# Latent attention's shifts found by whole pairs, half of them between the differential heads, and a features-first layout for the first layer's inputs

## The chip, the cores and the metric

The kernel runs on one core of a Trainium2 chip. The metric is the device time in microseconds of one execution. Engines: PE (TensorE: matrix products and transposes into the banks of PSUM), DVE (VectorE), ACT (ScalarE), POOL (GpSimd) and SP (SyncE), which here issues all transfers. Each engine works through its own queue in order; semaphores tie the queues together.

## The reference

Two layers over 1024 latent tokens and 256 context tokens of width 1024. Each layer modulates the tokens with a scale and a shift that come from a conditioning vector, projects them, mixes them with two groups of heads, gates and projects back, and normalises. The first layer is the one the change touches:

```python
sh_l, sc_l, g_l = adaln(c, ada_w[l], ada_b[l])      # silu(c) @ ada_w + ada_b, in three parts
hl = xl * (1.0 + sc_l[:, None]) + sh_l[:, None]
hc = xc * (1.0 + sc_c) + sh_c                       # context tokens
...
# 4 differential heads: two softmaxes over the same keys, subtracted
p = softmax(q1 @ k1.T * DA_SCALE) - lam * softmax(q2 @ k2.T * DA_SCALE)
oa = rms_norm(p @ vd) * subln_g * (1.0 - lam_init)
# 8 latent (MLA) heads, 96 features of query and key
ob = softmax(qm @ km.T * MLA_SCALE) @ vm
y = concat([oa, ob]) * silu(gate)
```

Latent tokens see all 1280 keys, context tokens only the 256 of the context.

## The kernel before

**Stages.** The start (0 to 67 us) loads the conditioning weights, tokens and the first input weights, and builds the modulated tokens as `hhi` and `hlo`, a rounded part and a remainder, with features on the partitions. Then come the first layer's projections, which leave queries, keys, values and gates in memory (`s_qk`, `s_v`, `s_mq`, `s_mk`, `s_kr`, `s_mv`, `s_gate`), its attention (about 460 to 1012 us), its output projection, and the second layer.

**The start.** `load_x` brings tokens in with tokens on the partitions (`xt`), and `modulated` (L279) turns each 128x128 block on PE (L285) before ACT scales and shifts it (L287) and DVE writes the two parts (L289, L290). `ada_first` (L250) makes scale and shift from a block of `ada_w`, 128 columns of each, which arrive as runs of 128 numbers (512 bytes). Small vectors (`c`, biases, gains) come as rows, a transfer for each, and are turned on PE in `load_rows` (L188).

**The attention.** `Plan` (L504) holds tasks with engine, cost, predecessors and the buffers that they take and give. `run` picks the task that can start first by these costs (`on_vector`, `on_scalar`) and emits it; so the costs set the order on every engine, but not the times on the chip. Two kinds of unit are planned:

- `Differential` (L563), one head each, 4 in all, for 8 tiles of 128 queries and one context step. For each tile and each of the two softmaxes PE writes scores of 128 x 1280 into a wide PSUM tile `s` of three banks (L565, L566), DVE finds the row maximum (L1329), and ACT takes the exponential (L1336). DVE scales and combines the two (L579, L580, L585) in pieces of 512, 512 and 256; PE turns the result in blocks of 128 (L1353), ACT or DVE moves the blocks out (`moves`, L518), and PE multiplies by the values (L596). There are two `s` tiles and two single banks `tp`.
- `Latent` (L752), two heads each, 4 pairs in all, in groups of 4, 4 and 2 tiles. Here the scores are made turned, keys on the partitions (`st`, L862 to L864), ACT takes their exponential (L878) at once, and PE multiplies by the values (L898). DVE and POOL add up the probabilities (L889), PE sums them over the keys (L906), and DVE takes the reciprocal (L913) and gates. Since nothing can be subtracted behind the product, the row maximum has to be inside it, as feature 97 of the query's remainder (`ql`, row 96), against a row of ones in the keys.

**The shift.** This maximum is found by `Latent.shifts`, a group ahead of its use: a rough product with the rounded parts alone (L789) into an `s` tile, the maximum on DVE (L797 into `nmx`), one-column transposes of `nmx` on PE (L805), and a copy on ACT into the row of `ql` (L810). The score product of a group waits for it. In the latent stage one wide `s` tile is left, and three single banks `st`.

**Queues.** SP issues the loads of the next head or pair (`load_scores`, `load_values`), the stores, the steps of `bias_tables` and the weights of what follows, in the order of the plan. A load into a buffer that is still in use waits on SP, and so does everything behind it. Units use two sets of buffers in turn.

Of the kernel before, what the change touches and what calls it, by code (L numbers as in the profile page):

```python
# [53 lines left out]
RD = 1  # L54
RM = 1
# [80 lines left out]

@with_exitstack
def hybrid_kernel(ctx, tc, t, out, dbg=None):
# [11 lines left out]
    dma(out=cst, in_=t["cst"])  # L150
# [11 lines left out]
    s_mv = dram.tile([NT, 512], F32, name="s_mv")  # L162
    s_gate = dram.tile([KT, P, NT], F32, name="s_gate")
# [21 lines left out]
    V0 = {}  # L185
    V1 = {}

    def load_rows(spec, where, dst, rows, psum, n=0):  # L188
        n0 = n
        G.memset(rows, 0.0)  # L190
        for key, ap, off, k in spec:
            dma(out=rows[n:n + k, :], in_=row_of(ap, off, k))
            where[key] = n
            n += k
        assert n <= P
        ps = psum.tile([P, 512], F32, name="mm")
        T.transpose(ps[:, :P], rows, ident)
        V.tensor_copy(out=dst[:, n0:n], in_=ps[:, n0:n])

    rows_pool = ctx.enter_context(space(name="rows", bufs=1))  # L200

    def vec_rows0(pool, psum):
        rows = pool.tile([P, P], F32, name="rows")
        load_rows([("c", t["c"][0], 0, 8), ("cc", t["c_ctx"], 0, 8)], V0, vt[0], rows, psum)
# [4 lines left out]
    def vec_rows1(psum):  # L209
        ada_b = t["ada_b"]  # L210
        spec = [("ab0", ada_b[0], 0, 16), ("ab1", ada_b[1], 0, 16),
                ("eg", t["ev_b_in"][0], 1952, 8), ("sub", t["da_subln_g"][0], 0, 1),
                ("qg", t["mla_q_norm_g"][0], 0, 2), ("kg", t["mla_kv_norm_g"][0], 0, 1)]
        rows = rows_pool.tile([P, P], F32, name="rows")
        load_rows(spec, V0, vt[0], rows, psum, 16)
# [274 lines left out]

    def on_vector(n):
        return 0.07 + n / 960

    def on_scalar(n, act=True):
        return (0.15 if act else 0.06) + n / 1200
# [15 lines left out]
    def moves(plan, bank, dst, m, last, cut=3):  # L511
# [10 lines left out]
        return [plan.add("AV", (on_scalar((c1 - c0) * P, False), on_vector((c1 - c0) * P)), partial(move, c0=c0, c1=c1),  # L522
# [8 lines left out]
    class Differential(Unit):  # L531
# [22 lines left out]
        def plan(self, tt):  # L554
# [26 lines left out]

            def combine(cs):
                def emit(_):
# [169 lines left out]
    class Latent(Unit):  # L753
# [24 lines left out]
        def shifts(self, plan, g):  # L778
# [58 lines left out]
            if n * w <= 512:  # L837
                return [context]
# [1733 lines left out]
```

## Time and profile before

| | us |
|---|---|
| median of 3 runs | 1938.26 (1933.92 to 1942.24) |
| profiled execution | 1938.62 |
| its span | 1936.9 |
| PE busy | 1803.0 |
| DVE busy | 1128.5 |
| ACT busy | 728.3 |
| POOL busy | 513.1 |

Busy times of matrix products overlap, since one starts before the one ahead of it has left the array; a busy PE is not PE at its peak. The granted clock of PE is 0.966 over the whole span. "Releasers" in the views name the work that ended an idle time. DVE's and ACT's busy times add up without overlap.

### The profile page before, as it was taken

The numbers are of one execution on the slowest core, as the hardware profiler recorded it, in microseconds if no ns is written. First come the engines' busy times: TensorE is split into PE (matmuls) and PEld (weight loads), VectorE is DVE, ScalarE is ACT, GpSimd is POOL, SyncE is SP. The second block draws the span as 40 slices with busy tenths as digits, with TensorE's granted clock in tenths as the row PEclk, the third lists the DMA queues.
The fourth block names the chain that finished last, engine by engine and source line by source line (L and its number), as shares of the span: only waits on it lengthen the run. The fifth ranks groups of instructions, "written<-read, shape, count | busy, mean of one in ns | idle before, by whom it ended". The sixth has DMA issues, their size and how long they took to land.

```text
span 1936.9 us, 29600 instructions
## 1 busy us (share of the span) xinstructions
PE 1803.0 (93%) x11085; PEld 1504.4 (78%) x11085; DVE 1128.5 (58%) x2116; ACT 728.3 (38%) x1451; POOL 513.1 (26%) x531
## 2 busy tenths in 40 slices
PE   7999999999898889889899989999999998998898
PEld 5898998887787766556557779888898877877786
DVE  3654124314889886676676853665676224666756
ACT  2311014434777545334342312334543224444521
POOL 1433134100012104436233422220111002223444
PEclk9999999999999979899899989999999999999999
DMA  9766524677654265422116342225442366677652
GB/s 288 237 199 217 163 72 126 188 203 184 145 125 107 66 152 156 125 67 62 42 55 209 131 148 74 80 74 185 146 134 84 109 193 172 159 204 191 176 163 87
DMA packets 241589, 275.97 MB, mean 142 GB/s; under 512 B 25042, under 2 KB 201118, under 8 KB 241446
## 3 DMA queue, kind: packets, MB, share of 16 engines
q1 hardware_dynamic: 241446, 274.07, 49.2%
q8 instruction: 88, 1.44, 0.3%
q14 instruction: 55, 0.45, 0.1%
HBM read 193.14 MB, written 87.16 MB: 145 GB/s over the span
## 4 chain that ended last, share of the span: by engine, by line
PE 59%; DVE 11%; DMA 5%; issue 3%; ACT 3%; POOL 1%; SPq 1%; DVEq 0%; POOLq 0%; ACTq 0%
PE mm L390 6%; PE mm L392 6%; PE mm L391 6%; PE tp L898 4%; PE tp L596 3%; PE mm L1985 3%; PE mm L1986 2%; PE mm L1987 2%; PE st L862 2%; PE st L864 2%; PE st L863 2%; PE s L789 2%; PE tp L1353 2%; DVE nm L1329 2%; PE s L565 2%
## 5 line engine op out<-in xcount | busy, mean ns | idle before, releaser
L347 POOL TENSOR_TENSOR wlo<-raw,whi 128x1024 fp32r<-128x1024 f32 (+2 forms) x38 | 91.7, 2414 | 210.7 <-ACT whi L339 207.4
L390 PE MATMUL mm<-whi,hhi 128*128 128x256 f32 (+1 forms) x496 | 147.5, 298 | 0.0
L392 PE MATMUL mm<-whi,hlo 128*128 128x256 f32 (+1 forms) x496 | 146.6, 296 | 0.2 <-DVE hlo L290 0.2
L391 PE MATMUL mm<-wlo,hhi 128*128 128x256 f32 (+1 forms) x496 | 146.4, 295 | 0.0
L1329 DVE TENSOR_REDUCE nm<-s 128x1 f32<-128x1280 f32 x64 | 94.6, 1489 | 53.0 <-PE s L566 51.5
L339 ACT CAST whi<-raw 128x1024 fp32r<-128x1024 f32 (+2 forms) x54 | 55.9, 1036 | 179.5 <-DMA raw<-in_ev_w_in_dram 70.6
L797 DVE TENSOR_REDUCE nmx<-s 128x1 f32<-128x1280 f32 x68 | 100.5, 1485 | 37.0 <-PE s L789 36.5
L2375 POOL TENSOR_SCALAR np<-np,nrz 128x640 f32<-128x640 f32 x64 | 52.0, 816 | 233.4 <-DVE nrz L2372 219.7
L1336 ACT ACTIVATE p<-s,nm 128x1280 f32<-128x1280 f32 x64 | 85.0, 1329 | 35.4 <-DVE nm L1329 30.9
L565 PE MATMUL s<-o 128*128 128x512 f32 (+1 forms) x192 | 79.8, 420 | 18.1 <-ACT p L1336 16.4
L390 PEld LDWEIGHTS mm<-whi,hhi 128*128 128x128 f32 x496 | 94.7, 191 | 2.1 <-issue 1.7
L392 PEld LDWEIGHTS mm<-whi,hlo 128*128 128x128 f32 x496 | 94.6, 191 | 0.5 <-DVE hlo L290 0.4
L391 PEld LDWEIGHTS mm<-wlo,hhi 128*128 128x128 f32 x496 | 94.7, 191 | 0.2
L1985 PE MATMUL mm<-h,whi 128*128 128x512 f32 x192 | 78.9, 411 | 3.3 <-DVE hv L2021 3.3
L789 PE MATMUL s<-o 96*128 96x512 f32 (+1 forms) x204 | 65.4, 430 | 17.8 <-DVE nmx L797 11.2
L878 ACT ACTIVATE pt<-st 128x512 f32<-128x512 f32 (+1 forms) x88 | 50.7, 578 | 75.1 <-PE st L864 70.9
L596 PE MATMUL tp<-v,pt 128*128 128x128 f32 x640 | 76.8, 276 | 0.7 <-ACT pt L518 0.2
L596 PEld LDWEIGHTS tp<-v,pt 128*128 128x128 f32 x640 | 74.4, 192 | 3.7 <-DVE pt L518 2.4
L1986 PE MATMUL mm<-h,whi 128*128 128x512 f32 x192 | 76.5, 398 | 0.0
L1987 PE MATMUL mm<-h,wlo 128*128 128x512 f32 x192 | 76.4, 398 | 0.0
L2368 ACT ACTIVATE np<-np,nnm 128x640 f32<-128x640 f32 x64 | 52.9, 827 | 56.4 <-DVE nnm L2362 51.0
L862 PE MATMUL st<-o 96*128 96x512 f32 (+1 forms) x176 | 73.1, 415 | 0.0
(488 smaller groups left out, 5370.1 us busy)
## 6 DMA issues: line engine op xcount, KB each, us to landing
adaw<-in_ada_w_dram SPq DMA_DIRECT2D x16, 1024.0 KB
raw<-in_od_w_in_dram SPq DMA_DIRECT2D x32, 512.0 KB
o<-s_qk SPq DMA_DIRECT2D x48, 320.0 KB
raw<-in_ev_w_in_dram SPq DMA_DIRECT2D x18, 512.0 KB
bt<-s_bt SPq DMA_DIRECT2D x16, 576.0 KB
adaw<-in_ada_w_dram SPq DMA_DIRECT2D x16, 512.0 KB
o<-s_mq SPq DMA_DIRECT2D x16, 480.0 KB
s_gate<-e SPq DMA_DIRECT2D x24, 256.0 KB
```

What stands on the lines that cost most here:

```text
L390: T.matmul(ps, ahi(k), bhi(k), start=k == k0, stop=False)
L391: T.matmul(ps, ahi(k), blo(k), start=False, stop=False)
L392: T.matmul(ps, alo(k), bhi(k), start=False, stop=k == nk - 1)
L565: T.matmul(s[:, n0:n0 + nn], ql, self.kh[b][:, ks], start=True, stop=False)
L596: T.matmul(o[:, :P], x["pt"][:, c, :], self.v[:, k0 + c, :], start=c == 0, stop=c == nch - 1)
L789: T.matmul(x["s", a, i][:, n0:n0 + nn], self.qh[a][0:96, (t0 + i) * P:(t0 + i + 1) * P], self.kh[a][0:96, k0 * P + n0:k0 * P + n0 + nn], s ...
L797: V.tensor_reduce(out=x["m", a][:, i:i + 1], in_=x["s", a, i][:, :w], axis=AX.X, op=ALU.max, negate=True)
L862: T.matmul(st[:, :nq], self.kh[a][0:96, ks], self.qh[a][0:96, qs], start=True, stop=False)
L1329: V.tensor_reduce(out=nm, in_=s[:, :w], axis=AX.X, op=ALU.max, negate=True)
L1985: T.matmul(ps, ah, bh, start=k == 0, stop=False)
L1986: T.matmul(ps, ah, bl, start=False, stop=False)
L1987: T.matmul(ps, al, bh, start=False, stop=k == KT - 1)
```

## The change

Three things are changed.

**1. Shifts.** `Latent.shifts` now works on one head `a` of a pair, over all ten tiles. It reads the rounded queries and keys from memory into tiles of its own: keys into the ring of weights (`whi` for the first, `wlo` for the second head of a pair), queries two tiles at a time into `rq` (three buffers, 40 loads). The maxima of both heads gather in `kept` (128 x 20); one transpose turns them, one copy moves them out, and one transfer writes them to `s_sh` in memory, from where `load_scores` brings the row of `ql` in. Hence a pair is loaded after its rows are written, and the score products wait for no shift of their own. There are 72 such steps in all. The first 36 (pairs 0 and 1) are planned one by one between the 36 steps of the differential heads, the other 36 between the score steps of pairs 0 and 1. Both wide `s` tiles exist from the start; one is given up for three `st` banks when the differential scores are done, and the other when the last shift step is done, for three more. The weights of the next layer begin to load only then. (Before, four steps of pair 0's first group were planned twice: 68 maxima over 1280 keys for 64 tiles.)

**2. Balance.** The middle piece of each combination (512 of 1280) goes from DVE to POOL, as two instructions; blocks that PE has turned are moved out by ACT alone; products over one `s` tile stay together; and the plan's costs of DVE and ACT are raised for this stage.

**3. Layouts.** The host hands over `tokens` (features first), `ada0` (the first layer's `ada_w` in blocks, so that half a block is a transfer of 4 KB runs), and `vectors0` and `vectors1` (small vectors as columns). The 80 transposes of tokens and the three of vectors are gone, and tokens come in 2 KB runs (1 KB for context).

```diff
+    tokens = np.concatenate([inputs["x"][0], inputs["ctx"][0]], axis=0)
+    out["tokens"] = np.ascontiguousarray(tokens.T)
+    w = inputs["ada_w"][0][:, 0:2 * D].reshape(KT, P, 2, KT, P)
+    out["ada0"] = np.ascontiguousarray(w.transpose(3, 1, 0, 2, 4).reshape(KT, P, KT * 2 * P))
...
-        return [plan.add("AV", (on_scalar((c1 - c0) * P, False), on_vector((c1 - c0) * P)), partial(move, c0=c0, c1=c1),
+        return [plan.add("A" if plan.name == "attention" else "AV", (on_scalar((c1 - c0) * P, False), on_vector((c1 - c0) * P)), partial(move, c0=c0, c1=c1),
...
+                    if eng is G:
+                        G.tensor_scalar(out=p2, in0=p2, scalar1=x["ratio"], scalar2=1.0, op0=ALU.mult, op1=ALU.mult)
+                        G.tensor_tensor(out=p1, in0=p1, in1=p2, op=ALU.add)
+                    else:
+                        V.scalar_tensor_tensor(out=p1, in0=p2, scalar=x["ratio"], in1=p1, op0=ALU.mult, op1=ALU.add)
...
+            for n0, nn in pieces(w):
+                eng, cost = ("G", 2.1) if n0 == 512 else ("V", 0.06 + on_vector(nn))
...
+            dma(out=self.ql[a][96:97, :].bitcast(F32), in_=s_sh[p][a:a + 1, :])
...
+        def shifts(self, plan, a):
...
+            def load_q(i):
                 def emit(_):
+                    x["q", i] = rough.tile([P, 256], FR, name="rq", bufs=RQ)
+                    dma(out=x["q", i][0:96, :].bitcast(F32), in_=s_mq[0][2 * self.p + a][:, i * 256:(i + 1) * 256])
...
+            def turn(_):
+                x["t"] = taken("tp")
+                T.transpose(x["t"][0:2 * TILES, 0:P], self.kept.rearrange("p a t -> p (a t)"), ident)
...
+                self.shift.append(plan.add("V", on_vector(n * w), top(tt, n), last, [], ["s"], rank=RM))
+                if tt + n == TILES and a == 1:
+                    last = plan.add("P", 0.2, turn, self.shift, ["tp"])
+                    last = plan.add("A", on_scalar(P, False), rows, [last], ["yd"], ["tp"])
+                    self.rows = plan.add("D", 1.0, store, [last], [], ["yd"])
+            return loading, [partial(step, tt, 1) for tt in range(LT)] + [partial(step, LT, 2)]
...
-                    m = plan.add("P", 3 * nq / 2250, block(c, a), [self.ready[a], self.shift[g, a]], ["st"],
+                    m = plan.add("P", 3 * nq / 2250, block(c, a), [self.ready[a]], ["st"],
...
+                h = xp.tile([P, 512], F32, name="h", bufs=3)[:, :n * P]
+                S.activation(out=h, in_=xs[g, k // 2][:, k % 2, :], func=AF.Identity,
...
+        usual = dict(fixed)
+        fixed.update(V=0.15, copy=0.16)
...
+            after = [u.rows] if u in mla else []
...
+        parts_left = [(j, step) for j, (_, steps) in enumerate(ahead) for step in steps]
+        parts_later = parts_left[9 * EARLIER:]
+        parts_left = parts_left[:9 * EARLIER]
...
+                for j, step in parts_left[:-(-len(parts_left) // units_left)]:
+                    step()
...
+                for j, later in parts_later[:1]:
+                    later()
...
+                    if len(parts_later) == 1:
+                        plan.add("P", 0.01, banks, [plan.tasks[-1]], ["s"], ["st"] * 3)
+                        spread(plan, w1.begin(), [plan.tasks[-2]])
```

Line numbers in the rows of after are those of the changed file: L830 is the rough product, L839 its maximum, L888 to L890 the score products, L610 the combination on DVE, L607 and L608 that on POOL.

On PE, where pair 0 ends and pair 1 begins, before stood the values (L898) and sums (L906) of the last group, rough products into the one wide tile (`s_4838`), four one-column transposes, a rough product more, and then the scores:

```order
L898 MATMUL tp_4840<-p_4841,v 64x256 x2
L898 MATMUL tp_4840<-pt_4847,v 64x256 x2
L906 MATMUL tp_4839<-oo,cst 64x256 x2
L789 MATMUL s_4838<-o_7004 128x512 x2
L789 MATMUL s_4838<-o_7004 128x256
L805 MATMUL tp_4839<-cst,nmx 1x128 x4
L789 MATMUL s_4838<-o_7054 128x512 x2
L789 MATMUL s_4838<-o_7054 128x256
L862 MATMUL st_7098<-o_7004 128x512
```

Now, at the same place, the sums (L932) stand between score products of the next pair (the other operands `o_7803` and `o_7741` are its loaded tiles):

```order
L888 MATMUL st_7083<-o_7741 128x512
L889 MATMUL st_7083<-o_7741 128x512
L890 MATMUL st_7083<-o_7741 128x512
L932 MATMUL tp_4715<-oo,cst 64x256 x2
L888 MATMUL st_7081<-o_7803 128x512
L889 MATMUL st_7081<-o_7803 128x512
L890 MATMUL st_7081<-o_7803 128x512
```

The transposes and the rough products ahead of the first scores are gone from between the pairs.

On DVE, in a differential head, a tile before was two maxima, the ratio and three pieces (`x2` are the first two):

```order
L1329 TENSOR_REDUCE nm<-s_4856 128x1
L1329 TENSOR_REDUCE nm<-s_4838 128x1
L579 RECIPROCAL ratio<-zs 128x1
L580 SCALAR_TENSOR_TENSOR ratio<-ratio,r_5354,nlam 128x1
L585 SCALAR_TENSOR_TENSOR p_4843<-p_4844,ratio,p_4843 128x512 x2
L585 SCALAR_TENSOR_TENSOR p_4843<-p_4844,ratio,p_4843 128x256
```

Now two pieces are left of the combination, and the maximum of a latent tile (`kept`) follows them:

```order
L1355 TENSOR_REDUCE nm<-s_4713 128x1
L1355 TENSOR_REDUCE nm<-s_4709 128x1
L598 RECIPROCAL ratio<-zs 128x1
L599 SCALAR_TENSOR_TENSOR ratio<-ratio,r_5299,nlam 128x1
L610 SCALAR_TENSOR_TENSOR p_4717<-p_4718,ratio,p_4717 128x512
L610 SCALAR_TENSOR_TENSOR p_4717<-p_4718,ratio,p_4717 128x256
L839 TENSOR_REDUCE kept<-s_4713 128x1
```

A piece of 512 has left DVE and a reduction over 1280 has come in its place.

On SP, in the differential heads, the loads of queries for the shifts (`rq`) now stand between the table's transfers (L1411), the loads of the next head's values and gate (L569, L571), a store of a pair's rows (L854) and the stores of the heads (L770):

```order
L822 DMA rq<-s_mq_70 96x256
L854 DMA s_sh_77<-yd 20x128
L569 DMA v<-s_v 128x10x128
L571 DMA gt<-s_gate 128x1280
L770 DMA s_y<-yd 128x512
L822 DMA rq<-s_mq_70 96x256 x2
```

A query load behind the gate's load (L571) or a store (L770) is issued only when these have been.

More of the change, by code (lines that the diff above doesn't have):

```diff
@@ L162, in hybrid_kernel @@
     s_mv = dram.tile([NT, 512], F32, name="s_mv")
+    s_sh = [dram.tile([2, NT], F32, name=f"s_sh{p}") for p in range(4)]
     s_gate = dram.tile([KT, P, NT], F32, name="s_gate")
@@ L183, in hybrid_kernel, with vectors, vec_rows0 @@
     subg = subgt[:, 0:1]
[L185 to L204, printed above, removed]
+    V0, V1 = [places(spec)[0] for spec in VECTORS]
+    def vectors(i, n0, n1):
+        dma(out=vt[i][:, n0:n1], in_=t[f"vectors{i}"][:, n0:n1])
+    def vec_rows0():
+        vectors(0, 0, 16)
         G.memset(sil, 0.0)
@@ L207, in vec_rows0, with vec_rows1 @@
         S.activation(out=sil[:, :, 1], in_=vt[0][:, 8:16], func=AF.Silu)
[L209 to L215, printed above, removed]
+    def vec_rows1():
+        vectors(0, 16, places(VECTORS[0])[1])
         V.tensor_scalar(out=subgt, in0=vt[0][:, V0["sub"]:V0["sub"] + 1], scalar1=1.0 - (0.8 - 0.6), scalar2=None,
@@ L580, in scale, with emit @@
                 V.scalar_tensor_tensor(out=ratio, in0=ratio, scalar=x["z", 0], in1=nlam, op0=ALU.mult, op1=ALU.mult)
+            x["left"] = len(pieces(w))
             def combine(cs):
[L583 removed]
+                def emit(eng):
                     p1, p2 = x["p", 0][:, cs], x["p", 1][:, cs]
[L585 to L586 removed]
+                    if eng is G:
[3 more added lines that the diff above has]
+                        V.scalar_tensor_tensor(out=p1, in0=p2, scalar=x["ratio"], in1=p1, op0=ALU.mult, op1=ALU.add)
+                    x["left"] -= 1
+                    if not x["left"]:
                         given("p", x["p", 1])
@@ L776, in load_values, with load @@
             dma(out=self.gate, in_=s_gate[4 + p])
-        def shifts(self, plan, g):
-            t0, n = TG[g]
-            k0, w = keys_of(t0)
+        def shifts(self, plan, a):
             x = {}
-            self.shift = getattr(self, "shift", {})
-            def rough(a, i, n0, nn):
+            def load(_):
+                x["k"] = ring[0].tile([P, KT, WC], FR, name=("whi", "wlo")[a]).rearrange("p k n -> p (k n)")[:, :NT]
+                dma(out=x["k"][0:64, :].bitcast(F32), in_=s_mk[0][self.p, 64 * a:64 * a + 64, :])
+                dma(out=x["k"][64:96, :].bitcast(F32), in_=s_kr[0])
+            def load_q(i):
@@ L848, in shifts @@
-            return [partial(step, a, i) for a in range(2) for i in range(n)]
+                    if self.kept is None:
+                        self.kept = at.tile([P, 2, TILES], F32, name="kept", bufs=2)
+                    w = keys_of(tt)[1]
+                    V.tensor_reduce(out=self.kept[:, a, tt:tt + n], in_=x["s", tt][:, :n * w].rearrange("p (m k) -> p m k", k=w),
+                                    axis=AX.X, op=ALU.max, negate=True)
+                    given("s", x["s", tt])
+                return emit
@@ L1478, in hybrid_kernel @@
                 loaded(mla[u.p + 1])
-            ahead = groups[i + 1][0].shifts(plan, groups[i + 1][1]) if i + 1 < len(groups) else []
-            steps = u.scores(plan, g)
-            for c, step in enumerate(steps):
+            for step in u.scores(plan, g):
                 first = len(plan.tasks)
```

198 lines of the change are left out of this document (102 added, 96 removed).

## The prediction

> **What bounds the kernel now.** The first view is the table by stage: busy time of each engine in each stretch, number of instructions in brackets, then the granted TensorE clock, the share of the DMA engines and what they moved.
>
> ```profile
> core 0: us, PE busy (x) PEld busy (x) DVE busy (x) ACT busy (x) POOL busy (x), PEclk, DMA share, GB/s
> 0.00:67.00 67.00, 51.95 (x429) 42.39 (x430) 28.29 (x69) 20.05 (x28) 11.49 (x17) 1.00 1.01 281
> 67.00:460.00 393.00, 388.99 (x2758) 356.68 (x2757) 131.82 (x279) 96.00 (x189) 107.55 (x133) 1.00 0.56 172
> 460.00:722.00 262.00, 227.93 (x1477) 194.33 (x1475) 219.28 (x336) 166.19 (x408) 34.01 (x62) 0.94 0.54 123
> 722.00:1012.00 290.00, 269.28 (x1213) 169.33 (x1213) 195.98 (x189) 120.91 (x216) 122.33 (x101) 0.93 0.31 87
> ```
>
> The change reaches three of these stretches. In the first 67 us the DMA share is 1.01: loading bounds it. From 67 to 460 the PE is busy for 389 of 393 us and nothing is changed there, so what the start gains is carried through. From 460 to 722 (differential heads) no engine is full; VectorE is the fullest by its own work. From 722 to 1012 (latent pairs) PE is idle for 20.7 us, and at a clock of 0.93 it loses another 0.07 x 290 = 20.3 us.
>
> Next I read who PE waited for in these two stretches (total, times, longest), and the clock at one change of pair.
>
> ```profile
> PE s L789 <- DVE nmx L797: 9.6, 7, 2.2
> PE tp L805 <- DVE nmx L797: 8.2, 7, 1.9
> PE tp L906 <- DVE rz L913: 2.7, 3, 0.9
> ...
> PE s L565 <- ACT p L1336: 16.4, 15, 1.9
> ...
> 864.00:877.00 13.00, 10.33 (x32) 7.54 (x33) 8.75 (x9) 2.96 (x5) 1.18 (x1) 0.61 1.03 252
> ```
>
> The first two rows (17.8 of the 20.7 us) are the shift: rough product, maximum on VectorE, transpose, row, and only then the first score product of the next group. They fall where one pair ends and the next begins, and there the clock goes down as well (0.61 in those 13 us). So the latent stage is bound by PE's own stream plus one serial chain that is paid at each change of pair.
>
> **Latent stage.** PE's stream is priced by starts, not by durations (these overlap).
>
> ```profile
> 774.91 0.40 PE L862 MATMUL st<-o 96*128 96x512 f32 x1
> 775.15 0.40 PE L863 MATMUL st<-o 96*128 96x512 f32 x1
> 775.38 0.40 PE L864 MATMUL st<-o 97*128 97x512 f32 x1
> ...
> 777.01 0.28 PE L862 MATMUL st<-o 96*128 96x256 f32 x1
> 777.13 0.28 PE L863 MATMUL st<-o 96*128 96x256 f32 x1
> ...
> 740.03 4.44 PE tp L898 x20
> ...
> L862 PE MATMUL st<-o 96*128 96x512 f32 x160 | 68.5, 428 | 0.0
> L898 PE MATMUL tp<-p,v 128*64 128x512 f32 x160 | 41.5, 597 | 0.0
> L789 PE MATMUL s<-o 96*128 96x512 f32 x96 | 36.7, 463 | 9.6 <-DVE nmx L797 9.6
> L805 PE MATMUL tp<-cst,nmx 128*1 128x128 f32 x65 | 12.3, 298 | 9.0 <-DVE nmx L797 8.2 <-DVE nmx L824 0.8
> L596 PE MATMUL tp<-v,pt 128*128 128x128 f32 x40 | 4.8, 275 | 0.0
> ```
>
> (Counts that no row here shows are of the same list.) A 512-column score product starts every 0.235 us, a 256-column one every 0.12, a value product every 4.44/20 = 0.222. What stays: 480 x 0.235 + 48 x 0.12 (scores) = 118.6; 320 x 0.222 + 32 x 0.12 (values) = 74.9; the sums, 32 x 0.235 + 12 x 0.12 = 9.0; the rest of the last differential head, 40 x 0.12 + 16 x 0.12 = 6.7. Together 209.2 us. Before there stood beside it 96 x 0.235 + 64 x 0.12 = 30.2 us of rough products and about 65 x 0.1 = 6.5 us of one-column transposes, in all 246. The other 44 of the 290 us are the idle time (20.7), the lost clock (20.3) and 3 us that I cannot place.
>
> After: half the rough products are gone from here. The 36 steps left (order of the change) are 32 of 2 x 0.235 + 0.12 = 0.59 us and 4 of 0.24, or 19.9 us; the transposes become 4, after a whole pair, and nothing in the next scores waits for them. So the stream is 209.2 + 19.9 = 229 us. Of the 44 us I leave 11: the 2.7 us for the reciprocal, the 3 unplaced and 5 of the lost clock, since the changes of pair keep their sums and their reciprocals. That makes **240 us, 50 less**. The ends: all 44 stay (273, 17 less), or none (229, 61 less). I lean to the lower end because the waits named are the ones removed. The 36 maxima here cost VectorE 36 x 1.49 = 54 us against 49 before; it is busy for 196 of 290 us, and PE's step of scores, values and rough product (6 x 0.235 + 4 x 0.222 + 0.59 = 2.9 us) covers one maximum, until VectorE falls behind: then PE waits, because only one wide bank is left for the rough products.
>
> **Differential stage.** An undisturbed head, with its groups on VectorE and ScalarE:
>
> ```profile
> 552.90:610.40 57.50, 51.69 (x368) 45.35 (x367) 48.82 (x83) 41.37 (x105) 8.02 (x18) 1.00 0.58 128
> ...
> L585 DVE SCALAR_TENSOR_TENSOR p<-p,ratio,p 128x512 f32<-128x512 f32 x16 | 11.6, 747 | 0.2
> L518 DVE COPY pt<-tp 128x256 f32<-128x256 f32 x7 | 2.9, 420 | 2.3 <-ACT pt L518 2.3
> L518 ACT COPY pt<-tp 128x256 f32<-128x256 f32 x36 | 12.0, 376 | 3.6 <-PE tp L1353 3.4
> ...
> L797 DVE TENSOR_REDUCE nmx<-s 128x1 f32<-128x1280 f32 x49 | 72.8, 1485 | 34.9 <-PE s L789 34.5
> L648 DVE TENSOR_REDUCE nmx<-s 128x4 f32<-128x1024 f32 x4 | 4.9, 1216 | 1.4 <-PE s L643 1.4
> ```
>
> VectorE works 48.8 of 57.5 us. The change takes from it, per head, 8 middle pieces of the combination (8 x 0.747 = 6.0) and 7 copies (2.9), and gives it 8 maxima (8 x 1.485 = 11.9) and one over 512 elements (between 0 and the 1.2 us of the 1024-element row; I take 0.7, near half): 52.5 us. ScalarE takes the copies, 41.4 + 7 x 0.376 = 44 us. PE gets 9 steps, about 5 us. The pieces that go to GpSimd are priced thus:
>
> ```profile
> L726 POOL TENSOR_SCALAR oo<-oo,rs 128x128 f32<-128x128 f32 x32 | 11.3, 372 | 1.0
> ...
> L2375 POOL TENSOR_SCALAR np<-np,nrz 128x640 f32<-128x640 f32 x64 | 52.0, 816 | 233.4 <-DVE nrz L2372 219.7
> ...
> L889 POOL TENSOR_TENSOR oo<-oo,p 128x512 f32<-128x512 f32 x34 | 47.0, 1381 | 46.0 <-ACT p L878 29.9 <-DVE oo L889 13.9
> ...
> 749.38 1.52 POOL L889 TENSOR_TENSOR oo<-oo,p 128x512 f32<-128x512 f32 x1 [0.17 <-ACT p L878]
> ...
> 749.98 1.48 DVE L889 TENSOR_TENSOR oo<-oo,p 128x512 f32<-128x512 f32 x1 [0.22 <-ACT p L878]
> ```
>
> A product with a scalar over 512 is about 0.70 us (between 0.372 and 0.816), an addition 1.38: 2.1 us per tile, 17 per head on an engine that works 8 of 57.5. That is free by itself. It isn't beside VectorE: the last two rows show an addition of VectorE that ran while GpSimd had one and took 1.48 us, about 0.73 more than the 0.747 of the combination alone. VectorE's two remaining pieces run in the same microseconds as GpSimd's two instructions. The price lies between 0 and 2 x 0.73 = 1.46 us per tile; I take 0.5, since the first piece starts before GpSimd and only the second can be held by the 0.70. So 8 x 0.5 = 4: 56.5 us of VectorE.
>
> [...]
>
> Now the idle part: 8.7 us per head today. With a third user of two wide banks more of it is filled, since the maxima need nothing but a bank; I take 6, so 62.5 us per head (ends: 57.5, all new work in today's gaps; 52.5 + 11.7 + 8.7 = 73). Four heads are 250 us against 262, in which the last head already carried 20 rough steps and its own change to the latents: **12 less** (32 less to 30 more).
>
> **The start.**
>
> ```profile
> DMA packets 22994, 15.49 MB, mean 310 GB/s; under 512 B 494, under 2 KB 22990, under 8 KB 22990
> ...
> 70.00:80.00 10.00, 9.06 (x71) 8.35 (x72) 10.00 (x21) 2.49 (x4) 7.69 (x12) 1.00 1.08 359
> ...
> PE tr L197 <- DMA rows<-in_mla_kv_norm_g_dram: 4.4, 1, 4.4
> ...
> 22.54 0.64 PE L285 MATMUL tr<-cst,xt 128*128 128x128 f32 x4
> ```
>
> From 10 to 60 us the DMA engines move 15.49 MB at 310 GB/s, nearly all of it in packets under 2 KB. The new layouts give 4 KB and 2 KB rows. At the 359 GB/s of the second row the same bytes take 43.1 us, 6.9 less. The 80 token transposes (0.12 us each, 9.6 us) stand beside loading and pay nothing until loading is faster; then they no longer stand in its way. PE's second wait (4.4 us, small rows ahead of the first modulation) is shortened too, but the first big load must land first: 1 us. **8 less** (0, if PE's chain sets the pace, to 14, with the whole 9.6 and 4.4).
>
> **Sum.** The profiled execution took 1938.62 us (span 1936.9; the median of the runs is 1938.26, so it stands for them). 1938.6 - 8 - 12 - 50 = 1868.6, so 1869.
>
> **Rivals.**
> *GpSimd holds VectorE.* For it: 1.48 us. Against it: the order of the pieces. With both pieces held, VectorE has 52.5 + 11.7 = 64.2 and a head is 70 us: 280 instead of 262. Time: 1938.6 - 8 + 18 - 50 = 1899. Chance 0.17.
>
> *The waits change places.* PE waits for the one wide bank, behind a late VectorE, for as long as it waited for the maxima (17.8 us): 1869 + 18 = 1887. For it: a maximum of 1.49 us and its bank stand in 36 of 88 score steps, in an order that can't give way. Against it: 196 of 290 us of VectorE. Chance 0.10.
>
> *The clock stays low* at the changes of pair: 15 us of the lost 20.3 come back, 1869 + 15 = 1884 (with the rival above, 1902). Against it: the clock was 1.00 in the head above, with PE at 51.7 of 57.5 us, and 0.61 where PE had 10.3 of 13; less idle time should lift it. Chance 0.07. [...]
>
> *The small loads come late* (the slower side). 40 loads of queries, through three buffers, stand in one queue on SP behind loads and stores that wait:
>
> ```profile
> SPq L776 <- DVE yd L736: 36.1, 1, 36.1
> SPq L741 <- DVE yd L736: 32.2, 4, 10.3
> SPq L552 <- DVE yd L736: 23.7, 2, 12.6
> ```
>
> PE runs in order, so a late load stops everything behind its rough step. Three buffers of two steps give a lead of about three tiles, 3 x 7 = 21 us, which hides all of these waits but the longest. If the lead were lost, the 92 us would reach PE: 1869 + 92 = 1961. It decides from 79 us on (1948). Chance 0.04.
>
> *All ends are good*: 1938.6 - 14 - 32 - 61 = 1832; chance 0.07, from 1850 down.
>
> **Numbers.** The forecast (1850 to 1882) has 0.55. Range 1838 to 1910: the three rivals above it and a part of the good one inside, only the late loads and the far good end out. A measurement tells about 0.5% (10 us) from no change: faster 0.92, same 0.04, slower 0.04.
>
> **What would show it.** Start: the first input product of the second weights some 8 us earlier and over 340 GB/s. Heads: 60 to 65 us, and the last combination piece near 0.48 us or, wrong, above 1. Latents: no PE wait for a maximum in front of a transpose, a clock over 0.97, 235 to 245 us. Wrong: PE waits for a query load, or a latent stage over 265 us.

## The result, and the profile after

| | before | after |
|---|---|---|
| median, us | 1939.86 (4 runs) | 1879.57 (4 runs, 1876.76 to 1881.52) |
| ratio, 95% interval | | 0.969 (0.967 to 0.972) |
| profiled execution, us (its span) | 1938.62 (1936.9) | 1881.52 (1879.9) |
| start and projections: to the first maximum of a differential tile | 460.5 | 457.5 |
| differential stage: from there to the first latent score | 261.7 | 258.1 |
| latent stage: from there to the start of its last sum product | 291.5 | 239.4 |
| the rest of the span | 923.2 | 924.9 |

The change is 60 us faster by the medians, where 70 were forecast; 1879.6 lies inside the range (1838 to 1910) and inside the forecast's own (1850 to 1882). The stages are cut at the same events in every kernel from here on. Of the 57 us between the two profiled spans, 52.1 are the latent stage, 3.6 the differential stage, 3.0 the start; the rest gives back 1.7. The rest is not touched by the change and lies between 918 and 928 us in all profiles below, so 2 us there mean nothing.

In the table by stage, after (columns as in the prediction: length, busy time of the engines, PE's granted clock, DMA share, GB/s), the two stages read:

```profile
457.47:715.60 258.13, 224.64 (x1499) 197.33 (x1498) 216.65 (x293) 165.52 (x427) 101.83 (x121) 0.97 0.53 126
715.60:955.02 239.42, 236.05 (x1101) 145.98 (x1100) 192.29 (x161) 112.38 (x206) 147.80 (x117) 1.00 0.50 134
```

In the latent stage PE is idle for 3.4 of 239 us (before: 21.9 of 291.5), at a clock of 1.00 (0.93). The waits of PE (total, times, longest), first those of the differential stage, then all of the latent stage:

```profile
PE s L830 <- ACT p L1362: 9.7, 11, 1.7
PE s L830 <- DMA rq<-s_mq: 8.3, 3, 3.7
PE s L584 <- ACT p L1362: 7.9, 11, 1.9
PE s L584 <- DVE kept L839: 4.1, 5, 1.7
...
PE tp L932 <- DVE rz L939: 2.5, 1, 2.5
PE tp L1379 <- POOL p L608: 0.8, 2, 0.6
```

No product waits for a maximum of its own shift any more. In the differential stage PE waits for a wide tile `s`: until ScalarE's exponential has read it (9.7 + 7.9) or the maximum of a latent tile has (4.1). Three loads of queries were late (8.3).

One execution of the kernel of e3 (4410 us) and one of before beside e5 (2538 us) were disturbed and are left out, and the profile of e3's kernel is therefore the one of e5.

### The profile page after: what moved, and what is told of

Its sections match the earlier page's. It is cut to its first block, busy times and chain, and to the rows that moved or that the text cites. A ratio compares the mean times of both kernels' runs of the same rounds, so it can differ in the third digit from the quotient of the medians.

```text
span 1879.9 us, 29391 instructions
## 1 busy us (share of the span) xinstructions
PE 1761.8 (94%) x10910; PEld 1476.5 (79%) x10910; DVE 1122.1 (60%) x2041; ACT 721.6 (38%) x1460; POOL 608.6 (32%) x602
## 4 chain that ended last, share of the span: by engine, by line
PE 54%; DVE 10%; DMA 9%; ACT 3%; issue 3%; POOL 2%; SPq 2%; DVEq 0%; POOLq 0%; ACTq 0%
PE mm L407 5%; PE mm L409 5%; PE mm L408 5%; PE tp L924 3%; PE mm L2030 3%; PE mm L2031 3%; PE mm L2032 3%; PE tp L622 2%; PE st L888 2%; PE st L890 2%; PE st L889 2%; PE s L584 2%; PE s L830 2%; PE s L585 1%; ACT p L1362 1%
## 5 line engine op out<-in xcount | busy, mean ns | idle before, releaser
L1355 DVE TENSOR_REDUCE nm<-s 128x1 f32<-128x1280 f32 x64 | 94.2, 1488 | 58.6 <-PE s L585 57.5
L839 DVE TENSOR_REDUCE kept<-s 128x1 f32<-128x1280 f32 (+1 forms) x72 | 100.4, 1396 | 17.8 <-PE s L830 16.5
L584 PE MATMUL s<-o 128*128 128x512 f32 (+1 forms) x192 | 75.2, 393 | 12.8 <-ACT p L1362 7.9
L607 POOL TENSOR_SCALAR p<-p,ratio 128x512 f32<-128x512 f32 x32 | 31.5, 985 | 129.7 <-DVE ratio L599 110.8
L537 ACT COPY pt<-tp 128x256 f32<-128x256 f32 x168 | 55.0, 380 | 43.2 <-PE tp L1379 42.6
```

Source lines behind the costliest of these rows:

```text
L584: T.matmul(s[:, n0:n0 + nn], ql, self.kh[b][:, ks], start=True, stop=False)
L839: V.tensor_reduce(out=self.kept[:, a, tt:tt + n], in_=x["s", tt][:, :n * w].rearrange("p (m k) -> p m k", k=w), axis=AX.X, op=ALU.max, neg ...
L1355: V.tensor_reduce(out=nm, in_=s[:, :w], axis=AX.X, op=ALU.max, negate=True)
```

## The experiments

The theory at the outset: most of the gain is the serial chain at the changes of pair, the moved products are the smaller part; and in the differential stage the two wide tiles set the pace, so that the balance is worth little. The rivals: PE is full in the latent stage, and the gain is the work that left it; VectorE's work sets a differential head. All stages by the same cuts (in the differential stage PE's idle time is length less busy time):

| run | against | median, us | ratio to before (95%) | differential: us | VectorE busy | PE idle | clock | latent: us | clock |
|---|---|---|---|---|---|---|---|---|---|
| before | | | 1 | 261.7 | 219.5 | 34.3 | 0.94 | 291.5 | 0.93 |
| after | | 1879.6 | 0.969 (0.967, 0.972) | 258.1 | 216.7 | 33.5 | 0.97 | 239.4 | 1.00 |
| e1 even | before | 1915.3 | 0.990 (0.987, 0.992) | 264.5 | 221.2 | 35.7 | 0.95 | 268.0 | 0.97 |
| e2 layouts | before | 1929.1 | 0.997 (0.996, 0.998) | 261.7 | 219.6 | 34.4 | 0.94 | 291.4 | 0.93 |
| e3 unbalanced | after | 1915.2 | 0.990 (0.987, 0.992) | | | | | | |
| e4 rq4 | after | 1878.1 | 0.971 (0.969, 0.973) | 258.9 | 216.6 | 34.2 | 0.97 | 239.3 | 1.00 |
| e5, as e3 | after | 1913.4 | 0.988 (0.985, 0.990) | 293.8 | 236.0 | 47.9 | 0.92 | 242.1 | 0.99 |
| e6 nocosts | after | 1876.3 | 0.968 (0.967, 0.970) | 253.8 | 216.2 | 26.2 | 0.97 | 236.8 | 1.00 |
| e7 nopool | e6 | 1896.3 | 0.979 (0.975, 0.983) | 273.9 | 231.1 | 36.3 | 0.94 | 240.4 | 0.98 |
| e8 nomoves | e6 | 1893.7 | 0.977 (0.974, 0.980) | 267.0 | 244.1 | 35.4 | 0.98 | 241.4 | 0.99 |
| e9 earlier6 | after | 1911.9 | 0.988 (0.985, 0.990) | 287.0 | 240.1 | 41.8 | 0.95 | 239.7 | 0.98 |
| e10 pool2 | after | 1874.3 | 0.969 (0.967, 0.971) | 266.1 | 204.0 | 33.8 | 0.96 | 234.2 | 1.00 |
| e11 pool2, nocosts | e6 | 1879.4 | 0.972 (0.969, 0.975) | 257.7 | 201.6 | 29.9 | 0.99 | 239.5 | 0.99 |
| e12 earlier3 | e6 | 1869.9 | 0.965 (0.962, 0.967) | 242.4 | 202.9 | 26.0 | 0.96 | 248.0 | 1.00 |

The medians of before that were taken beside these runs lie between 1933.7 and 1939.9 us, so two rows are compared by their ratios, and by their medians only to some us.

**e1, the chain alone.** The kernel before, shift steps spread evenly and farther ahead:

```diff
-            ahead = groups[i + 1][0].shifts(plan, groups[i + 1][1]) if i + 1 < len(groups) else []
+            if i == 0:
+                later = [(v, f) for v, h in groups[1:] for f in v.shifts(plan, h)]
...
-                k = len(ahead) if c + 1 == len(steps) else -(-len(ahead) // (len(steps) - c))
-                for f in ahead[:k]:
-                    f()
-                ahead = ahead[k:]
+                if later and hasattr(later[0][0], "ready"):
+                    later.pop(0)[1]()
```

> The kernel before, with one thing altered: the shift steps of the latent pairs stand one behind each score step, as far ahead as the loads of their pair allow, instead of a group ahead. All 68 maxima, all rough products and all one-column transposes stay in the latent stage, and layouts and balance are as before. Theory (the chain): the latent stage became 50 us shorter mostly because the serial chain at a change of pair (rough product, maximum, transpose, row, first scores) is gone, with its waits of 17.8 us and the lost clock of 20.3 us; the moved products are 17 of the 50. Then this kernel gains about 30 us: 1909 (1900 to 1918), latent stage about 260 us of 292, clock above 0.97 there, hardly a wait of PE for nmx. Rival (the moved work): PE is full in this stage and the gain is the work that left it. Then it gains under 10 us: 1930 to 1940.

In the table by stage of e1, the latent stage, and ahead of it the 13 us in which before had a clock of 0.61:

```profile
864.00:877.00 13.00, 13.00 (x63) 7.65 (x62) 11.68 (x11) 5.36 (x9) 8.69 (x7) 1.00 1.03 250
...
724.21:992.20 267.99, 258.39 (x1208) 160.20 (x1206) 208.93 (x185) 120.24 (x213) 132.95 (x105) 0.97 0.34 93
```

PE's waits in the latent stage of e1 (total, times, longest):

```profile
PE s L789 <- DVE nmx L797: 5.5, 4, 2.7
PE st L862 <- ACT pt L878: 2.6, 1, 2.6
```

With every product kept the stage is 23.5 us shorter, 268.0 instead of 291.5; by the medians the kernel gains 18 us. That is the chain, and more than the rival's 10, though less than the 30 expected: PE still waits for the one wide tile (5.5). The first row covers the same microseconds as the row of 0.61 before, with the same load on the DMA engines (1.03 and 250 GB/s, against 1.03 and 252): PE has no gap there now, and the clock is 1.00. So here the load on the DMA engines doesn't go with the low clock. The stretch with the low clock had gaps of PE (2.7 of 13 us), but gaps don't always bring it: in after PE is busy for 8.92 of the 11 us from 640 to 651, at a clock of 1.00.

Where the other 28.6 us went is seen when each PE instruction of the latent stage is given the time from its start to the next start (worked out from the traces; waits and a low clock are inside):

| us in the latent stage | before | e1 | after | e9 | e12 |
|---|---|---|---|---|---|
| scores | 130.4 | 133.1 | 122.3 | 129.1 | 121.6 |
| values | 79.8 | 79.5 | 77.3 | 80.3 | 77.3 |
| rough products | 44.0 | 33.2 | 21.7 | 11.4 | 27.2 |
| transposes of maxima | 15.2 | 5.2 | 0.1 | 0.1 | 0.1 |
| sums over the keys | 15.2 | 10.4 | 10.9 | 10.3 | 10.6 |
| tail of the last differential head | 7.2 | 7.0 | 7.8 | 8.9 | 11.6 |

From e1 to after, 16.6 us are rough products and transposes that left, and 10.8 are scores, which no longer wait or run at a low clock: 7.0 of them are idle time behind a score, and the clock rises from 0.97 to 1.00. Whether this comes from the products that left or from the other things that differ (rows by way of memory, three more `st` banks) no run separates.

**e2, the layouts alone** (the features-first tokens, `ada0` and the vectors of the diff above, put into the kernel before):

```diff
-            dma(out=x, in_=src[r0:r0 + n * P, q * 256:(q + 1) * 256].rearrange("(a p) n -> p a n", p=P))
+            dma(out=x, in_=t["tokens"][q * 256:(q + 1) * 256, t0 * P:(t0 + n) * P].rearrange("(k p) n -> p k n", p=P))
...
-                        dma(out=w[:, :, i * P:(i + 1) * P], in_=src[:, :, i * D + f * P:i * D + (f + 1) * P])
+                        dma(out=w[:, ks], in_=t["ada0"][f].rearrange("p (k n) -> p k n", k=KT)[:, ks])
```

> The kernel before with the layouts alone (tokens features first, ada_w in blocks, vectors as columns); shifts and balance as before. In the changed kernel the first product with the second weights came 6 us earlier, but the attention only 3 us earlier. Theory: the layouts give the 6 us and lose 2 to 3 of them at once, since PE then waits for VectorE's remainders (hlo) and small preparations until about 95 us; so this kernel is 3 to 4 us faster, 1936, and first attention product 3 us earlier. Rival: the layouts give all of 6 to 8 us, and what was lost is due to the other parts (tiles that the attention lays out elsewhere): 1932 to 1934, attention 6 us earlier. A gain under 1 us would say that the start was not bound by loading.

By the ratio 3 to 8.5 us are gained, by the medians 4.6; the first maximum of a differential tile comes 6.2 us earlier. By the place of the attention the rival holds; by the medians the gain lies between the two. My reason for a loss of 3 us behind the start was wrong: in this kernel nothing is lost there. The start of the attention lies between 454.3 and 458.2 us in all profiles with the new layouts, against 459.8 and 460.5 without, so after's 457.5 lies inside that spread; whether its 3 us to e2 are chance or belong to the kernel is not shown.

**e3 and e5, without the balance.** The changed kernel with the second part of the change undone (only the products of a rough step still stay together):

```diff
-                    if eng is G:
-                        G.tensor_scalar(out=p2, in0=p2, scalar1=x["ratio"], scalar2=1.0, op0=ALU.mult, op1=ALU.mult)
-                        G.tensor_tensor(out=p1, in0=p1, in1=p2, op=ALU.add)
-                    else:
-                        V.scalar_tensor_tensor(out=p1, in0=p2, scalar=x["ratio"], in1=p1, op0=ALU.mult, op1=ALU.add)
+                    V.scalar_tensor_tensor(out=p1, in0=p2, scalar=x["ratio"], in1=p1, op0=ALU.mult, op1=ALU.add)
...
-        return [plan.add("A" if plan.name == "attention" else "AV", (on_scalar((c1 - c0) * P, False), on_vector((c1 - c0) * P)), partial(move, c0=c0, c1=c1),
+        return [plan.add("AV", (on_scalar((c1 - c0) * P, False), on_vector((c1 - c0) * P)), partial(move, c0=c0, c1=c1),
...
-        fixed.update(V=0.15, copy=0.16)
```

> The changed kernel without the balance: the combination all on VectorE in three pieces, turned blocks moved out by ScalarE or VectorE, the plan's old costs, no grouping of the products over one wide tile. Shifts and layouts as changed. Theory (the banks set the pace): in the differential stage PE waits for one of two wide tiles to come free, not for VectorE's total; the balance is worth little: 1880 to 1890, differential stage 260 to 270 us. Rival (the terms of the prediction): VectorE's total sets a head; it has 6.0 + 2.9 - 2.9 (the 0.37 us by which each of eight pieces is held up now) = 6 us more a head, so 24 us more: 1900 to 1908, differential stage 280 to 288 us.

> The kernel without the balance again, for its profile: it took 1915 us, 36 us more than the changed kernel, so the theory that the wide tiles alone set the pace has fallen. Theory (VectorE's work): a head has VectorE busy for 58 to 62 us instead of 54 and idle for about 10 as now, so the differential stage is 285 to 295 us and the latent stage stays near 240. Rival (the order): VectorE is busy for 58 us or less and the loss is idle time, since the old costs and ungrouped products give an order in which PE holds wide tiles for longer; then PE's waits in the differential stage grow by over 20 us, or the latent stage is over 245 us.

The theory of the banks fell, and e3's rival (1900 to 1908) was too low as well: 1915.2 in the first measurement (ratio 0.990, 0.987 to 0.992), 1913.4 in the second, some 35 us over after. The differential stage of e5 in the table by stage:

```profile
456.56:750.38 293.82, 245.88 (x1483) 208.75 (x1482) 235.99 (x349) 162.69 (x405) 34.47 (x66) 0.92 0.48 111
```

PE's longest waits in that stage (L818 is the rough product there, L582 the score, L827 the latent maximum):

```profile
PE s L818 <- ACT p L1350: 20.2, 13, 1.9
PE s L582 <- DVE kept L827: 14.9, 12, 2.4
PE s L582 <- ACT p L1350: 7.3, 6, 1.9
```

VectorE has 19.3 us more to do and the stage is 35.7 us longer. Its work is 59.0 us a head, as e5's theory had it (58 to 62), but its idle time did not stay near 10: it went from 10.4 to 14.5 us a head. So 16 of the 36 us are idle time of VectorE and not its work. What PE waits for is a wide tile, as after, but now 14.9 us of it are waits for a maximum of VectorE (4.1 after). PE is idle for 14.4 us more, and at a clock of 0.92 instead of 0.97 it loses up to another 16 us (an estimate: 0.08 x 293.8 less 0.03 x 258.1). The attention (both stages) takes 535.9 us, against 532.5 in e1, where all the shift work stays behind: **without the balance, moving half the shifts gains nothing over spreading them.**

**e4, a fourth buffer for the queries** (`RQ = 4`).

> The changed kernel with four buffers instead of three for the queries of the shift steps. The waits of PE for query loads were 8.3 us in the differential stage. Theory: they are real stops, and with a longer lead most of them go: 3 to 7 us faster than the changed kernel's 1879.6, 1873 to 1877. Rival: a wide tile sets the pace, and PE waits for that instead: 1879 to 1881, the 8.3 us turning into waits for ScalarE's p or VectorE's kept.

The time is no different, but neither expectation was put to the test: the wait for query loads is still 7.9 us (8.3), so a longer lead by one buffer doesn't reach what delays them. The trace of after shows where the three loads stood. SP issued them at 527.61, 579.64 and 595.13 us, each behind six loads of the next head (L562 to L564, 320 KB each) and three steps of the table (L1411), and PE went on 5.4, 7.4 and 6.1 us later. The DMA engines were full meanwhile or just before (a share of 1.07 from 519 to 527 us, 1.08 from 580 to 587). That the transfers ahead held them is the likely reading; an order with the query loads in front was not tried.

**e6, e7, e8, the balance by parts.** e6 leaves out the raised costs, e7 also the pieces on GpSimd, e8 (instead) ScalarE's copies:

```diff
-        fixed.update(V=0.15, copy=0.16)
...
-                ex.append(plan.add("A", on_scalar(w) + 0.25, exps(b), [last], ["p"], ["s"], rank=RANK))
+                ex.append(plan.add("A", on_scalar(w) + 0.1, exps(b), [last], ["p"], ["s"], rank=RANK))
```

```diff
-                eng, cost = ("G", 2.1) if n0 == 512 else ("V", 0.06 + on_vector(nn))
+                eng, cost = ("V", 0.06 + on_vector(nn))
```

```diff
-        return [plan.add("A" if plan.name == "attention" else "AV", (on_scalar((c1 - c0) * P, False), on_vector((c1 - c0) * P)), partial(move, c0=c0, c1=c1),
+        return [plan.add("AV", (on_scalar((c1 - c0) * P, False), on_vector((c1 - c0) * P)), partial(move, c0=c0, c1=c1),
```

> The changed kernel with the plan's old costs for this stage alone; middle pieces on GpSimd, copies on ScalarE and grouping as changed. VectorE's work is that of the changed kernel. Theory (VectorE's work): 1878 to 1886. Rival (the order): it loses a large part of the 36 us, 1895 or more.

> The changed kernel with the plan's old costs and with the middle piece of the combination back on VectorE; copies on ScalarE and grouping as changed. Theory (VectorE's work): against e6_nocosts VectorE has 6.0 us a head more and is held up 2.9 less, 3 us a head, or 12 us in all: 1890 to 1898. Rival (GpSimd's pieces cost as much as they take): within 4 us of e6_nocosts, or faster. Second rival (VectorE's waits for GpSimd go as well, but the whole 6 us come back): 24 us over e6_nocosts.

> The changed kernel with the plan's old costs and with the turned blocks moved out by ScalarE or VectorE, as the plan likes; middle pieces on GpSimd and grouping as changed. Theory (VectorE's work): the copies are 2.9 us a head, so up to 12 us over e6_nocosts: 1888 to 1898. Rival (the plan gives VectorE copies only where it is idle): within 4 us of e6_nocosts.

The differential stage in the table by stage, of e6:

```profile
455.10:708.94 253.84, 227.63 (x1510) 198.32 (x1508) 216.21 (x299) 164.78 (x432) 108.60 (x128) 0.97 0.55 128
```

Of e7, with the middle piece on VectorE:

```profile
456.92:730.86 273.94, 237.68 (x1529) 208.08 (x1528) 231.11 (x333) 168.17 (x437) 34.12 (x62) 0.94 0.51 120
```

Of e8, with copies on VectorE too:

```profile
455.35:722.39 267.04, 231.61 (x1531) 199.92 (x1530) 244.07 (x358) 152.51 (x374) 108.00 (x120) 0.98 0.53 122
```

The costs are worth nothing (1876.3 without them, 1879.6 with). The pieces on GpSimd are worth 20 us by the medians and by the stage, the copies 17 and 13. Together that is 37 by the medians, as much as e5 is slower than e6, and 33 of 40 by the stage. Both take work off VectorE, so this work counts. But its amount doesn't set the loss. In e7 15 us more of VectorE are 20 of the stage (the theory had 12 in all, the second rival 24): the clock falls from 0.97 to 0.94, and 4.0 us are one wait of PE for a copy on ScalarE (L850), not for VectorE. In e8 28 more are 13, with VectorE's idle time down from 37.6 to 23.0 us: many copies stand where it was idle. In e5 20 more are 40. The grouping of the score products, which e5 also undoes, was not tried alone.

**e9, three quarters of the shifts early** (`EARLIER = 6`).

> The changed kernel with 54 of the 72 shift steps among the differential tiles (two a step at first) instead of 36, and 18 in the latent stage instead of 36. Theory (VectorE's work sets a differential head): 18 maxima of 1.49 us, 27 us of VectorE, join the differential stage, which grows by 13 to 30 us (without the pieces on GpSimd 15 us more of VectorE were 20 us, without the moved copies 28 us were 13); the latent stage loses 18 x 0.59 = 10.6 us of PE: 1882 to 1899. Rival (the maxima fill idle time, and every product that leaves the full latent stage is a gain): 1869 to 1873.

Both stages of e9:

```profile
458.19:745.17 286.98, 245.17 (x1540) 211.53 (x1538) 240.08 (x317) 166.56 (x429) 109.43 (x129) 0.95 0.53 123
745.17:984.83 239.66, 231.23 (x1058) 141.74 (x1058) 171.11 (x142) 111.68 (x204) 140.32 (x103) 0.98 0.45 122
```

PE's waits in its latent stage:

```profile
PE tp L932 <- DVE rz L939: 2.5, 1, 2.5
PE tp L760 <- POOL oo L755: 2.1, 1, 2.1
PE st L888 <- ACT p L904: 1.7, 1, 1.7
```

23 us more of VectorE lengthen the differential stage by 29, at the end of what the theory had (13 to 30), and the median by 32 to 1911.9, where the theory had at most 1899. The surprise is the latent stage: 10.3 us of rough products left it and it is not shorter. By the table under e1 the scores take 6.8 us more, the values 3.0 and the tail 1.1: PE has gaps again (8.4 us idle, 3.4 after), and the clock is at 0.98. The likely reading is that the rough products had been filling waits for the other engines; no run tests it apart.

**e10 and e11, less work for VectorE.** The last piece goes to GpSimd too, with the changed and with the old costs:

```diff
-                eng, cost = ("G", 2.1) if n0 == 512 else ("V", 0.06 + on_vector(nn))
+                eng, cost = ("G", 2.1 if n0 == 512 else 1.2) if n0 >= 512 else ("V", 0.06 + on_vector(nn))
```

> The changed kernel with the last piece of the combination (256) on GpSimd as well, so that VectorE keeps one piece of three. Theory (VectorE's work sets a differential head): VectorE loses 32 x 0.68 = 22 us, and the differential stage 15 to 25 us: 1855 to 1865. Rival (a tile's own chain, or PE with its 225 us and ScalarE's exponentials, is now as late as VectorE): the pieces on GpSimd become some 1.3 us longer a tile, and nothing or up to 8 us is gained: 1872 to 1882.

> As e10_pool2, with the plan's old costs, which by themselves were no different from the changed ones. Theory and rival as there: 1852 to 1862, or 1870 to 1880.

The differential stage of e11:

```profile
457.88:715.61 257.73, 227.85 (x1509) 195.56 (x1508) 201.62 (x267) 165.32 (x432) 145.05 (x190) 0.99 0.54 126
```

Two of PE's waits in it:

```profile
PE s L584 <- ACT p L1362: 12.5, 18, 1.9
PE tp L1379 <- POOL p L608: 6.2, 12, 1.4
```

The rival holds for both: VectorE has 15 us less to do than in e6 and the stage isn't shorter. PE now waits for GpSimd's part of the combination (6.2 us, 1.4 in e6) and for wide tiles as before. In e10 that wait is 0.5 us and VectorE has 13 us less than after, yet the stage is 8 us longer. So this exchange has a knee, and the changed kernel stands at it. It doesn't show that less work of VectorE never helps, since the piece takes longer on GpSimd (0.51 + 0.74 us in e10, 0.66 on VectorE in after) and a tile's chain grows with it.

**e12, three eighths early** (`EARLIER = 3`, a pair's loads planned once its rows are; else e6):

```diff
-                loaded(mla[u.p + 1])
+                late = [mla[u.p + 1]]
...
+                if late and hasattr(late[0], "rows"):
+                    loaded(late.pop())
```

> As e6_nocosts (the changed kernel with the plan's old costs, 1876.3), with 27 of the 72 shift steps among the differential tiles instead of 36, and 45 in the latent stage; a pair is loaded once its rows are written. In e9_earlier6 18 more steps among the differential tiles cost 29 us there and gave nothing in the latent stage; in e10_pool2 less work of VectorE gave nothing. Theory (the differential stage stands at a knee: more work of VectorE lengthens it, less doesn't shorten it, and the latent stage is full of PE work): the differential stage gains at most 5 us, the latent stage loses 9 x 0.59 = 5.3: 1874 to 1883. Rival (a straight line from e9): the differential stage gains 13 to 15 us: 1864 to 1870. Second rival (the pairs' rows and loads come too late now): PE waits at the first change of pair, 1885 or more.

Its two stages:

```profile
457.42:699.85 242.43, 216.46 (x1432) 189.46 (x1430) 202.90 (x287) 163.25 (x422) 105.10 (x120) 0.96 0.57 134
699.85:947.87 248.02, 244.78 (x1169) 154.85 (x1168) 193.24 (x183) 113.28 (x210) 125.48 (x102) 1.00 0.47 129
```

The differential stage is 11.4 us shorter than in e6 and the latent stage 11.2 longer; 4.4 of each are value products of the last differential head that now stand behind the first latent score. What is left, 7.0 gained and 6.8 lost, is somewhat over the theory (at most 5, and 5.3) and short of the rival's 13 to 15; PE's listed waits in the latent stage are for the reciprocal alone, none for a load, so the second rival fell. Here VectorE has 13 us less to do than in e6, nothing went to GpSimd for it, and the stage does get shorter; but nine rough steps of PE (5.3 us) left it too, so which of the two did it is not shown. It comes out even: the two stages together are 490.5 us, in e6 490.7. The median is the lowest of all, 1869.9, below the theory's 1874 and at the end of the time that the rival gave (1864 to 1870), though the stages of the profile don't show the rival's gain. The profiled execution (1873.6) was the slowest of five; the interval of e12 overlaps that of e6. Whether it is a few us faster than e6 stays open; it is faster than before by 3.3 to 3.8%.

## Why the prediction was right, and where it was off

**The latent stage: right in size, and in the main in its reason.** Forecast 240 us and 50 less; measured 239.4 and 52 less. Leaning to the lower end, because the waits named were the ones removed, was right: e1 takes 23.5 us by spreading alone, and the products that left are 16.6 us from e1 to after, where the sum had 17 (30.2 + 6.5 - 19.9). By starts the stage is 240.1 us, that is the stream of 229 and 11 more, as forecast; but the 11 are made of other things, and that they fit is luck. I had left 5 us for the lost clock, and it was 1.00. The waits are 3.3 us, 2.5 of them the reciprocal (forecast 2.7). The other 7 to 8 are products that start a little later than priced: scores 122.3 (118.6), values 77.3 (74.9), rough products 21.7 (19.9). What I hadn't seen is that the moved products were a gain only down to about half: in e9 the same step of the sum, 0.59 us a rough step, bought nothing.

**The differential stage: the step that failed.** Forecast 12 less, measured 3.6. VectorE was forecast at 56.5 us a head; it is 216.65 / 4 = 54.2, so the work was over-priced by 2.3, 2 of them in the price of GpSimd's pieces (below). The idle part, "I take 6", was 10.4 (41.5 / 4), as large as in the stage before (42.2 / 4 = 10.5). I had let the maxima fill gaps because they need "nothing but a bank"; but the bank was short already. Before, in that stage, PE's waits for a wide tile were these, 25.9 us in all:

```profile
PE s L565 <- ACT p L1336: 16.4, 15, 1.9
PE s L789 <- ACT p L1336: 6.6, 4, 1.9
...
PE s L789 <- DVE nmx L797: 1.6, 3, 0.6
PE s L565 <- DVE nmx L797: 1.3, 2, 0.7
```

After they are 21.7, and 8.3 us for query loads have come on top, for which the idle part had nothing. How much of the miss is theirs can be read from e6: with the same work of VectorE (216.2) and no listed wait for a query load its stage is 4.3 us shorter (253.8), and VectorE is idle for 9.4 us a head. So about half of the 8.4 us missed may be the late loads; the rest is idle time that stays without them. The order of e6 differs in more than that, so this split is an estimate from the two profiles. The ends of the term were 57.5 and 73 for a head; 64.5 is inside.

The price of GpSimd's pieces, in the differential stage of after:

```profile
L610 DVE SCALAR_TENSOR_TENSOR p<-p,ratio,p 128x512 f32<-128x512 f32 x31 | 25.1, 809 | 0.7
L610 DVE SCALAR_TENSOR_TENSOR p<-p,ratio,p 128x256 f32<-128x256 f32 x31 | 20.5, 662 | 0.0
...
L608 POOL TENSOR_TENSOR p<-p,p 128x512 f32<-128x512 f32 x30 | 39.2, 1308 | 2.5
L607 POOL TENSOR_SCALAR p<-p,ratio 128x512 f32<-128x512 f32 x31 | 30.4, 979 | 129.6 <-DVE ratio L599 110.6 <-PE tp L1379 9.5 <-PE tp L622 3.7
```

VectorE's two pieces take 0.81 and 0.66 instead of 0.75 and 0.48 us: 0.25 us a tile, where I took 0.5. That 0.5 rested on the thought that only the second piece can be held, which no trace of before shows. In after a first piece 0.14 us ahead of GpSimd's product takes 0.75 (476.83 below), and two pieces in a row take 1.58 beside GpSimd's instructions (from 465.24) and 1.14 without them (from 473.74). The test that I named, 0.48 or above 1, gave neither; most pieces took 0.48 or 0.75, some 0.91. GpSimd's product was put at 0.70 and takes 0.98. The timeline of after shows why (start, us, what ran); in the first row VectorE is idle:

```profile
470.12 0.70 POOL L607 TENSOR_SCALAR p<-p,ratio 128x512 f32<-128x512 f32 x1 [2.16 <-ACT pt L537]
...
603.47 1.48 DVE L839 TENSOR_REDUCE kept<-s 128x1 f32<-128x1280 f32 x1
...
603.72 0.69 POOL L607 TENSOR_SCALAR p<-p,ratio 128x512 f32<-128x512 f32 x1 [6.77 <-DVE ratio L599]
...
476.83 0.75 DVE L610 SCALAR_TENSOR_TENSOR p<-p,ratio,p 128x512 f32<-128x512 f32 x1
...
476.97 1.18 POOL L607 TENSOR_SCALAR p<-p,ratio 128x512 f32<-128x512 f32 x1 [4.78 <-DVE ratio L599]
```

Alone it takes 0.70 and beside a maximum of VectorE 0.69; started 0.14 us behind VectorE's first piece it takes 1.18, 0.49 more. The other pieces of the stage agree: of 31, 8 ran beside a maximum (0.69 or 0.70), and 17 started 0.13 to 0.16 us behind a first piece (1.15 to 1.18). VectorE is ahead, as the order of the pieces had it, so here GpSimd pays. Records of VectorE overlap by some 0.08 us where one follows another (476.83 + 0.75, and the next at 477.50), those of ScalarE by some 0.1, so sums of durations run a little over the busy time.

**The start: right in kind, too large.** Forecast 8; the layouts alone gave 4.6 by the medians, 6.2 to the first differential maximum. The mis-sized term is in the main the rate. After:

```profile
10.00:55.00 45.00, 38.75 (x302) 29.74 (x303) 20.79 (x51) 14.81 (x18) 8.65 (x4) 0.96 0.92 336
```

15.49 MB at 336 instead of 359 GB/s are 46.1 us, 3.9 less than 50 where I had 6.9. The first input product of the second weights comes 6.1 us earlier (67.5 to 61.4), not 8. So 2.2 us are something else than the rate, where I had put 1 for PE's waits; what they are stays open.

**The rivals.** *GpSimd holds VectorE* fell (0.25 us a tile, not 1.46). *The waits change places* fell in the latent stage (no wait for the one wide tile). *The clock stays low* fell: 1.00. *The small loads come late* came true in kind: PE waits for a query load, which the prediction had named as a sign of being wrong. It is 8.3 us, far from the 79 from which it decides. In e5 the clock is 0.92 over the differential stage, in which no idle time of PE is longer than 2.4 us. The 1.00 from 640 to 651 us of after, with 2.1 us idle, shows that not each stretch with gaps is slow.

**The sum** was 1868.6 and the profiled execution took 1881.5: of the 13 us between, 8.4 are the differential stage and 5 the start, the rest of the span adds 1.7, and the latent stage takes 2 off.

**What stays open:** whether an order with the query loads in front would win back their 8.3 us; what the grouping of products is worth alone; whether a share between e12 and e6, or e12 with fewer gaps in the differential stage, is faster than 1869.9.

## What to carry to other kernels

Price a move of work by both stages: filler in a full-looking stage may be worth nothing to remove (e9: 10.3 us of rough products less, the latent stage 239.7 us against 239.4), and an engine with 16% idle time (VectorE after) can still cost time when it gets more to do (the differential stage is 20 us longer in e7 than in e6, 29 in e9 than after). The likely reason is that its instructions stand in the chain that frees a wide tile, for which PE waits (for VectorE's maximum 14.9 us in e5, 4.1 after). A serial chain paid at each change of unit can in part be removed by order alone (e1: 23.5 of 52 us, with no work moved). Where gaps come, count the clock with them: in e5 it cost, by the estimate above, up to as much as the gaps themselves (16 and 14 us).

## What the runs showed of the hardware

- The low clock at the changes of pair (0.61) is not tied to the loads that run there: with the same 250 GB/s and no gap of PE it is 1.00 (e1). Gaps alone don't fix it either: it was 1.00 in a stretch of after with PE idle for 2.1 of 11 us.
- In the differential stage of e5 the granted clock was 0.92, and no idle time of PE there was longer than 2.4 us.
- A product with a scalar on GpSimd (128x512) takes 0.69 or 0.70 us alone (2 in the differential stage of after) and beside a maximum of VectorE (8), and 1.15 to 1.18 when it starts 0.13 to 0.16 us behind a combination of VectorE (17). VectorE is busy in the last two cases, so in this stage the time goes with the instruction that runs beside it, not with VectorE being busy.
